# A two-layer S5 and convolution decoder on one core: the mixer's products in another order, weight units queued one unit later

## The chip, the core and the metric

The kernel runs on one core of one Trainium2 chip. The metric is the device time of one execution in microseconds, as the median of three runs; smaller is better.

## The reference

Two layers are computed for 288 tokens (256 of a prompt, 8 x 4 of a decode batch), with D_MODEL 2048, all in float32. The part that the change touches is the mixer of each layer:

```python
z = x @ w_in                                   # 2048 -> 1024 (u) + 1024 (cv) + 1024 (cg)
u, cv, cg = z[..., :1024], z[..., 1024:2048], z[..., 2048:]
y5, h_re, h_im = _s5(u, ...)                   # 64 groups x 16 channels, complex state of 64
g5 = gelu(y5)
s5_out = g5 * sigmoid(g5 @ s5_w_glu)
c = cv * sigmoid(cg)
c, new_conv = _causal_dwconv(c, conv_buf, conv_w, conv_b)     # width 31, per channel
c = silu(_ln(c, conv_ln_g, conv_ln_b))
mix = concatenate([s5_out, c]) @ w_out
x = _ln(ALPHA * x + mix, ln1_g, ln1_b)
```

A convolutional feed-forward net (2048 to 11264 and back) and an embedding product with layer norms follow. They are not changed.

## The kernel before

**Products.** Channels lie on the partitions, tokens on the free axis: x is 16 tiles of 128 x 288. Every weight matrix is cut into blocks of 128 x 128, stored in the order of use, and a block is used by three matmuls of 288 columns, since float32 is made of two halves: weight-high by x-high (L369), weight-high by x-low (L374), weight-low by x-high (L375). The first blocks of a group go in an order that uses the low halves last (L371, L351). `_order(matrix, ms, ks, g)` lists the blocks of a product for output chunks ms over input chunks ks, with g output chunks side by side for the first group; `run` (L343) walks such a list, and evicts an accumulator EV_GAP blocks after it is complete.

**Weights.** Eight blocks are a unit of 512 KB. `stream_dma` (L174) loads a unit into one of RAW_BUFS = 4 buffers `wraw`, on SP's queue (L179); `stream_hi` (L183) copies the high half to `whi` on ACT (L195); `stream_lo` (L199) makes `wlo` = wraw - whi on DVE and then queues the load of unit s + RAW_BUFS. This load can start when its buffer is free, that is after the `wlo` of the unit four before it. All operations of DVE are recorded in one line, L140, so the text goes by their tiles.

**The mixer** (L1051) computes first four chunks of u (phase u0), then for j = 0 to 7: the pair of cv and cg chunk j (phase p{j}, 32 blocks), the convolution of chunk j - 1 (`conv`, L1096), the DMAs for the convolution of chunk j (`stack`, L1070), and, where U_AT names one, one further chunk of u (phase v{j}, 16 blocks). A conv chunk goes through memory: DVE writes the gated product to `cbuf` (one buffer), POOL's queue writes cbuf to `cb_d` (L1136) and, after it, reads it back shifted in four DMAs into `stack` (L1078; the last chunk's on SP's queue), writes cbuf to the output (`out_dram`, L1080), and then loads the cached columns of the next chunk into cbuf (L1115). The convolution is 64 small matmuls on `stack` and `cw` (L1105, L1108).

**The scan** of the S5 runs beside this, chunk by chunk, as generators that `tick` steps between blocks. A chunk of u goes to memory (`u_d`) and comes back as `ust` (L799); `make_e` builds `em` from `sqb`, `sbt` and others (DVE, ACT); `bu` = ust by em and `project` = ust by tm and hin by om are small matmuls (both L389); between them kp goes to `k_d` and comes back as `tm` (L876); the result y goes to `y_d` and comes back in another order (L968), for the gelu. Loads are on SP's queue, which also carries the weights. When the generators step is decided when the program is built, by a model of TensorE's time: `pe_t` grows by 369 ns for each block and by 640 ns for each of a convolution's eight steps.

**The end of the mixer** is the glu product g (64 blocks; cut by G_CUT so that 32 blocks run ahead of the last convolution, 8 and 24 more beside its layer norm), then conv(7) and its layer norm (`ln_finish`, whose last matmul is L510, on the tile `ln_dg`), then the out product o: 256 blocks with 16 input chunks, k 0 to 7 from the scan and k 8 to 15 from the convolution, five output chunks side by side first.

Of the kernel before, what the change touches and what calls it, by code (L numbers as in the profile page):

```python
# [7 lines left out]
F32 = mybir.dt.float32  # L8
# [5 lines left out]
P = 128  # L14
# [12 lines left out]
CVC = 8  # L27
# [38 lines left out]
LOOK = 1  # L66
EV_GAP = 10
NATIVE = 10
G_CUT = (32, 40, 64, 64)
U_AT = {1: [4], 2: [5], 3: [6], 4: [7]}  # L70

# [22 lines left out]
def layer_phases():  # L94
    ph = [("u0", _order("w_in", range(4), range(KD), 4))]
    for j in range(CVC):
        ph.append((f"p{j}", _order("w_in", [8 + j, 16 + j], range(KD), 0)))
        if j in U_AT:
            ph.append((f"v{j}", _order("w_in", U_AT[j], range(KD), 0)))
    ph.append(("g", _order("s5_w_glu", range(8), range(8), 4)))  # L100
    ph.append(("o", _order("w_out", range(KD), range(KD), 5)))
    for z, ms in enumerate(EPARTS[:3]):
        ph.append((f"e{z}", _order("pe_w", ms, range(PEK), 0)))
    j0 = 0
    for h, n in enumerate(FH):
# [48 lines left out]
class Core:  # L154
# [44 lines left out]
    def stream_lo(self, upto):  # L199
        upto = min(upto, self.nblk // SB - 1)  # L200
        while self.next_lo <= upto:
# [8 lines left out]
            self.next_lo += 1  # L210
            self.stream_dma(s + RAW_BUFS)

# [129 lines left out]

    def run(self, blocks, xs, evac, sums=None, wide=False):  # L343

# [3 lines left out]
        for _, k, m in blocks:  # L348
# [17 lines left out]
            else:  # L366
                xh, xl = xs(k)
                self.pe_t += 369.0
                nc.tensor.matmul(out, w[0], xh, start=first, stop=False)  # L369
# [7 lines left out]
            if last:  # L377
                a, t = accs.pop(m)
                self.evq.append((a, lambda m=m, t=t: evac(m, t[:, :TOK])))
            if self.evq and self.pos - self.ev_pos >= EV_GAP:  # L380
                self.evict()
# [669 lines left out]
    def mixer(self, l, ph):  # L1051
        nc, a = self.nc, self.a
        V = self.V
        with self.tc.tile_pool(name="mx", bufs=1) as mp:
# [34 lines left out]
            def split_g(force=False, n=S5C):  # L1089
                while n and self.gdone and (force or self.gdone[0][1] <= self.pe_t):  # L1090
                    c = self.gdone.pop(0)[0]
                    self.split_x(8 + c, self.u32[c])
                    gsplit.add(c)
                    n -= 1

            def conv(j):  # L1096
                st, cw = stacks.pop(j)
                o = self.acc_tile()
                for k in range(8):
                    self.tick()  # L1100
                    self.pe_t += 640.0
                    if j == CVC - 2 and k >= 4:
                        split_g(n=1)
                    for b in range(4):
# [42 lines left out]

            def xs_g(k):
                split_g()
                while k not in gsplit:  # L1150
                    self.step(scan)
                    self.run_timed(True)
                    split_g(True)
                return self.xh[8 + k], self.xl[8 + k]
            def ev_g(m, acc):
                t = mp.tile([P, TOK], F32, tag="cvt", name="gt", bufs=3)
                nc.scalar.activation(t, acc, AF.Tanh, scale=0.25)
                w = mp.tile([P, TOK], F32, tag="cvt", name="gt", bufs=3)
                V.scalar_tensor_tensor(w.rearrange("p (n s) -> p s n", s=STEP),
                                       t.rearrange("p (s n) -> p s n", s=STEP), 1.0,  # L1160
                                       self.u32[m].rearrange("p (s n) -> p s n", s=STEP), op0=OP.add, op1=OP.mult)
                self.split_x(m, w, 0.25)
            sums = self.sums(ph["g"])
            self.run(ph["g"][:G_CUT[0]], xs_g, ev_g, sums)
            self.finish(scan)
            conv(CVC - 1)

            def fill(z):
                self.run(ph["g"][G_CUT[z]:G_CUT[z + 1]], xs_g, ev_g, sums)
            fill(0)  # L1170
            self.flush()
            self.ln_finish(cst, lambda z: z and fill(z), keep=True)
            th = {}

# [7 lines left out]
            def c_silu(j):  # L1182
# [4 lines left out]
                                          (3, lambda j: self.split_lo(8 + j, cvo[j], 0.5)))))  # L1187
            if G_CUT[2] < G_CUT[3]:
                fill(2)
            self.load_p(l, mp)  # L1190
            st = self.ln_begin(DM)

            def xs_o(k):
                self.need(min(k - 3, 7) - LOOK)
                return self.xh[k], self.xl[k]

            def ev_o(m, acc):
                V.scalar_tensor_tensor(self.x32[m], self.x32[m], 1.0 if m == KD - 1 else ALPHA, acc,
                                       op0=OP.mult, op1=OP.add)
                self.ln_acc(st, self.x32[m], m == KD - 1)  # L1200
                if m == 6:
                    self.ln_pre(st, self.x32[KD - 1], ALPHA)
            self.run(ph["o"], xs_o, ev_o, wide=True)
        return st

# [308 lines left out]
```

## Time and profile before

| | us |
|---|---|
| median of 3 runs | 2790.59 (2786.01 to 2801.34) |
| the profiled execution, its own time | 2793.7 |
| its span | 2791.9 |
| busy in the span: PE | 2684.0 (96%) |
| DVE | 1815.6 (65%) |
| ACT | 1353.2 (48%) |
| POOL | 304.3 (11%) |

The profiled execution has 1.8 us outside its span and is 3.1 us above the median. The profile is a page (busy time, 40 slices of the span, the chain that ended last, the costliest groups) and a trace that answers queries by window, engine and tile. Matmuls are pipelined, so the recorded duration of one (0.29 us) is longer than the distance between two. A wait is put down to whatever released it last.

### The profile page before, as it was taken

To read this page: it belongs to the slowest core of one execution; us is meant where nothing else is said; L and a number is where in the kernel's file an instruction comes from. 1 tells how busy PE (TensorE), PEld (TensorE's weight loads), DVE (VectorE), ACT (ScalarE), POOL (GpSimd) and SP (SyncE) were. 2 spreads that over 40 slices of the span, in tenths; PEclk is the share of its full clock that TensorE was granted. 3 is DMA by queue.
4 is the path that set the end of the run, shared out by engine and by line. 5 is a ranking of instruction groups with operands and counts; after the bars stand their busy time and mean duration, and the time that the engine had idled before them with its cause. 6 is when DMAs were issued, how large, how long until landed. Compare 5 with 4: busy or idle time off the path is not lost. (4 is left out here: it accounts for less than half of the span.)

```text
span 2791.9 us, 57891 instructions
## 1 busy us (share of the span) xinstructions
PE 2684.0 (96%) x23696; PEld 2623.0 (94%) x23696; DVE 1815.6 (65%) x3017; ACT 1353.2 (48%) x2224; POOL 304.3 (11%) x923
## 2 busy tenths in 40 slices
PE   8889999999999999999889879999999999999997
PEld 7778999999999999999888769999999999999997
DVE  6875768664566456667778747676645664566686
ACT  3444547553455345536454435475534553455363
POOL 3442001000000000000115410010000000000000
PEclk9999999999999999999999999999999999999998
DMA  7887544554455544544468874445555455455543
GB/s 238 240 237 224 171 152 164 162 181 163 158 168 164 180 159 157 181 162 151 145 197 242 225 206 156 150 161 165 180 166 162 159 179 171 150 173 171 166 152 102
DMA packets 175609, 487.72 MB, mean 175 GB/s; under 512 B 37616, under 2 KB 61696, under 8 KB 175344
## 3 DMA queue, kind: packets, MB, share of 16 engines
q1 hardware_dynamic: 160832, 434.56, 48.6%
q0 software_dynamic: 14512, 49.47, 6.4%
q8 instruction: 186, 3.05, 0.4%
q14 instruction: 79, 0.65, 0.1%
HBM read 463.27 MB, written 20.68 MB: 173 GB/s over the span
## 5 line engine op out<-in xcount | busy, mean ns | idle before, releaser
L369 PE MATMUL acc<-xh,whi 128*128 128x288 f32 x4656 | 1389.3, 299 | 13.0 <-ACT xh L528 5.1
L374 PE MATMUL acc<-xl,whi 128*128 128x288 f32 x4357 | 1289.7, 296 | 0.6 <-DVE xl L140 0.2
L375 PE MATMUL acc<-xh,wlo 128*128 128x288 f32 x4357 | 1284.3, 295 | 0.5 <-issue 0.5
L195 ACT ACTIVATE whi<-wraw 128x1024 fp32r<-128x1024 f32 x766 | 791.4, 1050 | 350.5 <-PE acc L374 220.4
L140 DVE TENSOR_TENSOR wlo<-wraw,whi 128x1024 fp32r<-128x1024 f32 x766 | 918.6, 1223 | 28.6 <-issue 12.5
L369 PEld LDWEIGHTS acc<-xh,whi 128*128 128x128 f32 x4656 | 876.5, 188 | 20.5 <-ACT xh L528 5.4
L374 PEld LDWEIGHTS acc<-xl,whi 128*128 128x128 f32 x4357 | 821.4, 189 | 3.7 <-DVE xl L140 2.1
L375 PEld LDWEIGHTS acc<-xh,wlo 128*128 128x128 f32 x4357 | 823.8, 189 | 0.7 <-issue 0.7
L140 DVE SCALAR_TENSOR_TENSOR fo<-fe,parf,fo 128x304 f32<-128x304 f32 x352 | 188.2, 535 | 354.2 <-ACT fo L1250 347.9
L369 PE MATMUL acc<-hh,whi 128*128 128x288 f32 x1408 | 416.4, 296 | 0.0
L374 PE MATMUL acc<-hl,whi 128*128 128x288 f32 x1312 | 387.7, 296 | 0.0
L375 PE MATMUL acc<-hh,wlo 128*128 128x288 f32 x1312 | 387.4, 295 | 0.0
L369 PEld LDWEIGHTS acc<-hh,whi 128*128 128x128 f32 x1408 | 264.9, 188 | 0.1
L375 PEld LDWEIGHTS acc<-hh,wlo 128*128 128x128 f32 x1312 | 247.2, 188 | 0.0
L374 PEld LDWEIGHTS acc<-hl,whi 128*128 128x128 f32 x1312 | 247.0, 188 | 0.0
L1246 ACT ACTIVATE fe<-acc 128x256 f32<-128x256 f32 x176 | 67.6, 384 | 301.1 <-PE acc L375 301.1
L1256 POOL COPY fstage<-fe 128x9 f32<-128x9 f32 x176 | 42.2, 240 | 1035.3 <-ACT fe L1247 1024.5
L428 ACT ACTIVATE ln_q<-x 128x288 f32<-128x288 f32 x90 | 40.2, 446 | 221.0 <-DVE x L140 221.0
L140 DVE TENSOR_TENSOR x<-x,acc 128x288 f32<-128x288 f32 x64 | 29.1, 454 | 144.7 <-PE acc L375 144.7
L1250 ACT ACTIVATE fo<-fe,parf 128x304 f32<-128x304 f32 x176 | 113.0, 642 | 16.5
L1270 ACT ACTIVATE hh<-fth 128x288 fp32r<-128x288 f32 x88 | 39.2, 445 | 162.9 <-DVE fth L140 162.9
L140 DVE SCALAR_TENSOR_TENSOR x<-x,acc 128x288 f32<-128x288 f32 x64 | 29.0, 453 | 132.9 <-PE acc L375 132.9
(237 smaller groups left out, 2366.9 us busy)
## 6 DMA issues: line engine op xcount, KB each, us to landing
wraw<-in_wts_dram SPq DMA_DIRECT2D x776, 512.0 KB
stack<-cb_d POOLq DMA_DIRECT2D x56, 282.0 KB, 8.8
cw<-in_convw_dram POOLq DMA_DIRECT2D x16, 512.0 KB, 5.7
cbuf<-in_convi_dram POOLq DMA_DIRECT2D x16, 283.5 KB, 4.5
cb_d<-cbuf POOLq DMA_DIRECT2D x16, 283.5 KB, 4.0
out_dram<-cbuf POOLq DMA_DIRECT2D x16, 283.5 KB, 10.4
tm<-k_d SPq DMA_DIRECT2D x64, 64.0 KB
sbt<-in_s5b_dram SPq DMA_DIRECT2D x14, 256.0 KB
```

The lines of the kernel that those rows point to most:

```text
L140: return f(out, *args, **kw)
L195: self.nc.scalar.activation(hi, self.raw[s], AF.Copy)
L369: nc.tensor.matmul(out, w[0], xh, start=first, stop=False)
L374: nc.tensor.matmul(out, w[0], xl, start=False, stop=False)
L375: nc.tensor.matmul(out, w[1], xh, start=False, stop=last)
L428: nc.scalar.activation(st["q"], v, AF.Square)
L1246: nc.scalar.activation(e[:, 2:2 + SEQ], acc[:, :SEQ], AF.Copy)
L1250: nc.scalar.activation(o[:, :w], e[:, 2:EW], AF.Identity, bias=self.prm("ffn_conv_b", m), scale=self.prm("ffn_conv_w2", m))
L1256: nc.gpsimd.tensor_copy(stage[:, z, :, 0], e[:, SEQ:EW:6])
L1270: nc.scalar.activation(hh[i], h, AF.Copy, scale=0.5)
```

## The change

The numbers of U_AT move two of the four u chunks that are computed between conv chunks one place forward (chunk 4 to j = 0, chunk 5 to j = 2) and the other two back (chunk 6 to j = 7, chunk 7 behind the last convolution, its first four blocks ahead of the layer norm's matmuls and twelve beside them). The out product is split: `oc` (input chunks 8 to 15, from the convolution, all output chunks, into ALPHA * x + result) runs right behind the convolution's layer norm, then g whole, then `os` (input chunks 0 to 7, added to x). The halves swap their tiles: the scan's chunks are split into tiles 0 to 7 for g, the glu's results into 8 to 15. HALF_GAP = 6 sets the evictions of oc and os. A weight unit is queued behind the `wlo` of the unit three before it, one unit later than before; its buffer comes free with the `wlo` of the unit four before it, as before. The model's `pe_t` grows by 400 ns for a block and 500 ns for a step of a convolution.

```diff
-G_CUT = (32, 40, 64, 64)
-U_AT = {1: [4], 2: [5], 3: [6], 4: [7]}
+HALF_GAP = 6
+U_AT = {0: [4], 2: [5], 7: [6]}
+U_END = 7
+V_CUT = (0, 4)
...
+    ph.append(("vz", _order("w_in", [U_END], range(KD), 0)))
+    ph.append(("oc", _order("w_out", range(KD), range(8, KD), 4)))
     ph.append(("g", _order("s5_w_glu", range(8), range(8), 4)))
-    ph.append(("o", _order("w_out", range(KD), range(KD), 5)))
+    ph.append(("os", _order("w_out", range(KD), range(8), 5)))
...
-            self.stream_dma(s + RAW_BUFS)
+            self.stream_dma(s + RAW_BUFS - 1)
...
-                self.pe_t += 369.0
+                self.pe_t += 400.0
...
-                    self.split_x(8 + c, self.u32[c])
+                    self.split_x(c, self.u32[c])
...
-                    self.pe_t += 640.0
-                    if j == CVC - 2 and k >= 4:
-                        split_g(n=1)
+                    self.pe_t += 500.0
...
+            conv(CVC - 1)
+            self.run(vz[V_CUT[0]:V_CUT[1]], self.xs, ev_u, vsum)
+            self.flush()
+            self.ln_finish(cst, lambda z: z and self.run(vz[V_CUT[1]:], self.xs, ev_u, vsum), keep=True)
...
+            def xs_c(k):
+                self.need(k - 8)
+                return self.xh[k], self.xl[k]
+
+            def ev_c(m, acc):
+                V.scalar_tensor_tensor(self.x32[m], self.x32[m], ALPHA, acc, op0=OP.mult, op1=OP.add)
+            self.run(ph["oc"], xs_c, ev_c, gap=HALF_GAP)
...
-            sums = self.sums(ph["g"])
-            self.run(ph["g"][:G_CUT[0]], xs_g, ev_g, sums)
+                self.split_x(8 + m, w, 0.25)
+            self.run(ph["g"], xs_g, ev_g)
             self.finish(scan)
-            conv(CVC - 1)
...
-            self.run(ph["o"], xs_o, ev_o, wide=True)
+            self.run(ph["os"], lambda k: (self.xh[8 + k], self.xl[8 + k]), ev_s, wide=True, gap=HALF_GAP)
```

SP's queue in layer 0, around the loads for the third chunk's scan (`wraw` a weight unit, `tm`, `sbt`, `sqb` the scan's tables, `u` the way back of y), before:

```order
L179 DMA wraw<-in_wts_dram 128x1024 x3
L876 DMA tm<-k_d 32x4x128 x4
L776 DMA sbt<-in_s5b_dram 128x512
L785 DMA sqb<-q_d 128x1x128 x4
L968 DMA u_2_182<-y_d 32x4x72 x4
```

and now:

```order
L183 DMA wraw<-in_wts_dram 128x1024 x2
L880 DMA tm<-k_d 32x4x128 x4
L183 DMA wraw<-in_wts_dram 128x1024
L780 DMA sbt<-in_s5b_dram 128x512
L789 DMA sqb<-q_d 128x1x128 x4
L972 DMA u_2_182<-y_d 32x4x72 x4
```

One of the three weight units that stood ahead of `tm` stands behind it.

SP's queue at the end of the same mixer, from the scan's sixth chunk on (`stack` is the last convolution's input), before:

```order
L968 DMA u_5_185<-y_d 32x4x72 x4
L179 DMA wraw<-in_wts_dram 128x1024 x3
L876 DMA tm<-k_d 32x4x128 x4
L179 DMA wraw<-in_wts_dram 128x1024
L968 DMA u_6_186<-y_d 32x4x72 x4
L179 DMA wraw<-in_wts_dram 128x1024 x4
L968 DMA u_7_187<-y_d 32x4x72 x4
L1078 DMA stack<-cb_d 32x4x564 x4
L179 DMA wraw<-in_wts_dram 128x1024 x8
```

and now:

```order
L972 DMA u_5_185<-y_d 32x4x72 x4
L183 DMA wraw<-in_wts_dram 128x1024 x5
L1082 DMA stack<-cb_d 32x4x564 x4
L183 DMA wraw<-in_wts_dram 128x1024 x4
L803 DMA ust<-u_d_3378 32x4x72 x4
L183 DMA wraw<-in_wts_dram 128x1024 x3
L803 DMA ust<-u_d_3552 32x4x72 x4
L183 DMA wraw<-in_wts_dram 128x1024 x6
L880 DMA tm<-k_d 32x4x128 x4
L183 DMA wraw<-in_wts_dram 128x1024 x2
L972 DMA u_6_186<-y_d 32x4x72 x4
```

The scan's last two chunks moved from ahead of the last `stack` to behind it.

DVE in layer 0, the last rows up to `xl_118`, the low half of the last conv chunk, which is the last input of its kind that the out product waits for (`cvo` a conv chunk, `ln_d` its normalised form, `xl` low halves; `sw`, `pw`, `bsm` tables of the scan), before:

```order
L140 TENSOR_TENSOR ln_d<-cvo_195,ln_s_4152 128x288
L140 SCALAR_TENSOR_TENSOR cvo_194<-ln_d,cvo_194 128x288
L140 SCALAR_TENSOR_TENSOR xl_116<-cvo_193,xh_100 128x288
L140 SCALAR_TENSOR_TENSOR cvo_195<-ln_d,cvo_195 128x288
L140 SCALAR_TENSOR_TENSOR xl_117<-cvo_194,xh_101 128x288
L140 TENSOR_TENSOR wlo<-wraw,whi 128x1024
L140 SCALAR_TENSOR_TENSOR xl_118<-cvo_195,xh_102 128x288
```

and now:

```order
L144 SCALAR_TENSOR_TENSOR cvo_194<-ln_d,cvo_194 128x288
L144 SCALAR_TENSOR_TENSOR xl_116<-cvo_193,xh_100 128x288
L144 TENSOR_TENSOR sw<-scc,aP 128x512 x2
L144 SCALAR_TENSOR_TENSOR cvo_195<-ln_d,cvo_195 128x288
L144 SCALAR_TENSOR_TENSOR xl_117<-cvo_194,xh_101 128x288
L144 TENSOR_TENSOR pw<-sw 128x4x64
L144 SCALAR_TENSOR_TENSOR pw<-sw 128x4x64
L144 TENSOR_TENSOR sw<-sbc,q 128x128 x2
L144 TENSOR_TENSOR bsm<-sw 64x4x16 x4
L144 TENSOR_TENSOR wlo<-wraw,whi 128x1024
L144 TENSOR_TENSOR sw<-bu,stb 128x576 x2
L144 SCALAR_TENSOR_TENSOR xl_118<-cvo_195,xh_102 128x288
```

Operations of the scan's last two chunks stand between the conv chunks now (four more, on `sqb` and `sw`, a little ahead of these rows); before, the scan was over here.

## Rows read from the trace of the kernel before

**Rows 1.** The page, busy time: engine, us, share of the span, instructions.

```profile
PE 2684.0 (96%) x23696; PEld 2623.0 (94%) x23696; DVE 1815.6 (65%) x3017; ACT 1353.2 (48%) x2224; POOL 304.3 (11%) x923
```

**Rows 2.** Windows: length, busy PE, PEld, DVE, ACT, POOL, clock, DMA share, GB/s.

```profile
61.00:306.00 245.00, 217.24 (x3511) 197.27 (x3512) 172.37 (x308) 104.52 (x199) 83.73 (x154) 0.97 0.80 230
600.00:1100.00 500.00, 500.00 (x3754) 500.00 (x3753) 277.94 (x383) 229.64 (x348) 23.92 (x146) 1.00 0.52 167
1392.00:1700.00 308.00, 268.80 (x3847) 245.34 (x3846) 214.44 (x383) 141.58 (x260) 90.19 (x165) 0.93 0.73 206
```

**Rows 3.** PE's waits from 1390 to 1700: us in total, times, the longest.

```profile
PE y L389 <- DMA wraw<-in_wts_dram: 7.6, 1, 7.6
PE acc L1105 <- DMA stack<-cb_d: 7.4, 1, 7.4
...
PE bu L389 <- DMA ust<-u_d: 5.2, 1, 5.2
PE acc L369 <- ACT xh L528: 5.1, 1, 5.1
PE y L389 <- DMA tm<-k_d: 3.1, 1, 3.1
PE bu L389 <- ACT em L815: 3.0, 3, 2.5
```

**Rows 4.** PE's waits from 55 to 306 (columns as in rows 3).

```profile
PE bu L389 <- ACT em L815: 8.4, 7, 3.6
PE bu L389 <- DMA ust<-u_d: 6.0, 2, 3.4
...
PE acc L1105 <- DMA stack<-cb_d: 2.1, 2, 1.3
```

**Rows 5.** Windows behind stalls (columns as in rows 2).

```profile
144.50:148.90 4.40, 4.09 (x72) 3.72 (x73) 4.32 (x13) 1.82 (x4) 0.58 (x1) 0.61 0.59 181
205.80:210.30 4.50, 4.50 (x102) 4.30 (x103) 1.60 (x3) 1.32 (x3) 1.57 (x3) 0.50 1.03 283
1455.60:1459.60 4.00, 4.00 (x66) 2.31 (x68) 2.75 (x5) 0.85 (x2) 1.09 (x2) 0.50 0.72 239
1640.30:1643.90 3.60, 3.60 (x98) 3.40 (x99) 0.00 (x0) 0.49 (x2) 0.47 (x1) 0.50 0.70 221
1668.40:1674.60 6.20, 6.19 (x52) 4.36 (x56) 3.29 (x7) 2.41 (x7) 0.00 (x0) 0.50 0.04 15
```

**Rows 6.** Timeline of SP's queue: start, us, instruction.

```profile
192.94 0.33 SPq L179 DMA_DIRECT2D wraw<-in_wts_dram  x1
193.37 2.06 SPq L876 DMA_DIRECT2D tm<-k_d  x4
```

**Rows 7.** Timeline of PE: start, us, instruction, idle time before and its end.

```profile
205.78 0.47 PE L389 MATMUL y<-ust,tm 128*32 128x72 f32 x8 [5.71 <-DMA sqb<-q_d]
...
281.26 0.64 PE L1105 MATMUL acc<-stack,cw 128*32 128x256 f32 x8 [1.29 <-DMA stack<-cb_d]
```

**Rows 8.** One convolution alone, by the tile stack (columns as in rows 2).

```profile
262.00:266.30 4.30, 4.17 (x128) 2.68 (x128) 0.00 (x0) 0.00 (x0) 0.00 (x0) 1.00 0.60 188
```

**Rows 9.** Timeline of POOL's queue, layer 0 (columns as in rows 7).

```profile
247.19 0.56 POOL L1136 DMA_DIRECT2D cb_d<-cbuf  x1 [4.78 <-DVE cbuf L140]
...
263.60 0.56 POOL L1115 DMA_DIRECT2D cbuf<-in_convi_dram  x1 [9.60 <-DMA out_dram<-cbuf]
...
267.94 0.54 POOL L1136 DMA_DIRECT2D cb_d<-cbuf  x1 [2.72 <-DVE cbuf L140]
```

**Rows 10.** Timeline of DVE behind the conv's layer norm (as in rows 7).

```profile
308.34 2.35 DVE L140 TENSOR_TENSOR wlo<-wraw,whi 128x1024 fp32r<-128x1024 f32 x2
310.61 0.82 DVE L140 TENSOR_TENSOR cvo<-cvo,ln_s 128x288 f32<-128x288 f32 x2
...
328.80 0.45 DVE L140 SCALAR_TENSOR_TENSOR xl<-cvo,xh 128x288 fp32r<-128x288 f32 x1
```

**Rows 11.** A group of DVE by shape, 61 to 306: busy us, mean ns.

```profile
L140 DVE TENSOR_TENSOR sw<-scc,aP 128x512 f32<-128x512 f32 x14 | 9.3, 692 | 14.6 <-DMA scc<-in_s5c_dram 13.3 <-ACT em L815 1.1
```

More of the change, by code (lines that the diff above doesn't have):

```diff
@@ L341, in sums, with run @@
         return tot, {m: 0 for m in tot}, {}
-    def run(self, blocks, xs, evac, sums=None, wide=False):
+    def run(self, blocks, xs, evac, sums=None, wide=False, gap=EV_GAP):
         nc = self.nc
@@ L379, in run @@
                 self.evq.append((a, lambda m=m, t=t: evac(m, t[:, :TOK])))
-            if self.evq and self.pos - self.ev_pos >= EV_GAP:
+            if self.evq and self.pos - self.ev_pos >= gap:
                 self.evict()
@@ L1146, in mixer @@
                     self.run(ph[f"v{j}"], self.xs, ev_u)
[L1148 to L1162, printed above, removed]
-            sums = self.sums(ph["g"])
-            self.run(ph["g"][:G_CUT[0]], xs_g, ev_g, sums)
-            self.finish(scan)
+            vz = ph["vz"]
+            vsum = self.sums(vz)
             conv(CVC - 1)
-            def fill(z):
-                self.run(ph["g"][G_CUT[z]:G_CUT[z + 1]], xs_g, ev_g, sums)
-            fill(0)
+            self.run(vz[V_CUT[0]:V_CUT[1]], self.xs, ev_u, vsum)
             self.flush()
-            self.ln_finish(cst, lambda z: z and fill(z), keep=True)
+            self.ln_finish(cst, lambda z: z and self.run(vz[V_CUT[1]:], self.xs, ev_u, vsum), keep=True)
             th = {}
@@ L1187, in mixer, with xs_g, ev_g, ev_s @@
                                           (3, lambda j: self.split_lo(8 + j, cvo[j], 0.5)))))
-            if G_CUT[2] < G_CUT[3]:
-                fill(2)
+            def xs_c(k):
[4 more added lines that the diff above has]
+            self.run(ph["oc"], xs_c, ev_c, gap=HALF_GAP)
+            def xs_g(k):
+                split_g()
+                while k not in gsplit:
+                    self.step(scan)
+                    self.run_timed(True)
+                    split_g(True)
+                return self.xh[k], self.xl[k]
+            def ev_g(m, acc):
+                t = mp.tile([P, TOK], F32, tag="cvt", name="gt", bufs=3)
+                nc.scalar.activation(t, acc, AF.Tanh, scale=0.25)
+                w = mp.tile([P, TOK], F32, tag="cvt", name="gt", bufs=3)
+                V.scalar_tensor_tensor(w.rearrange("p (n s) -> p s n", s=STEP),
+                                       t.rearrange("p (s n) -> p s n", s=STEP), 1.0,
+                                       self.u32[m].rearrange("p (s n) -> p s n", s=STEP), op0=OP.add, op1=OP.mult)
+                self.split_x(8 + m, w, 0.25)
+            self.run(ph["g"], xs_g, ev_g)
+            self.finish(scan)
             self.load_p(l, mp)
             st = self.ln_begin(DM)
[L1193 to L1199, printed above, removed]
+            def ev_s(m, acc):
+                V.tensor_tensor(self.x32[m], self.x32[m], acc, OP.add)
                 self.ln_acc(st, self.x32[m], m == KD - 1)
                 if m == 6:
-                    self.ln_pre(st, self.x32[KD - 1], ALPHA)
-            self.run(ph["o"], xs_o, ev_o, wide=True)
+                    self.ln_pre(st, self.x32[KD - 1])
+            self.run(ph["os"], lambda k: (self.xh[8 + k], self.xl[8 + k]), ev_s, wide=True, gap=HALF_GAP)
         return st
```

## The prediction

> **What bounds the kernel now.** I read the busy times first. PE is busy for 2684.0 of the 2791.9 us of the span [rows 1], so all waits of TensorE together are 108 us, and no reordering can bring more than these and what the clock loses behind them. Next the windows: from 600 to 1100, in the feed-forward net, PE is busy throughout, 3754 matmuls in 500 us, 0.133 us each, so a block of three takes 0.40 us and a weight unit 3.2 us [rows 2]. The two mixers are different: 27.8 us idle of 245 in layer 0 and 39.2 of 308 in layer 1, with a DMA share of 0.80 and 0.73 against 0.52, and DVE busy for 70% of both [rows 2]. 67 of the 108 us lie there, and that is where the change works. Third, what the waits are for: loads and tables of the scan (ust, tm, em), the conv stack, and in layer 1 the scan's last chunk [rows 3, 4]. Fourth, the clock: behind a stall of some 3 us or more, PE runs for a few us at its lower level, a granted clock of 0.50 (1.2 of 2.4 GHz), in layer 1 from 1455.6, 1640.3 and 1668.4, in layer 0 from 205.8, and in part (0.61) from 144.5 [rows 5]. A stretch of 4.0 us at 0.50 costs 2.0 us more.
>
> **What it takes away.** Same matmuls, in another order; the terms are waits.
>
> *The first convolution of layer 1* waits 7.4 us for its stack [rows 3]. Chunk 4 of u now stands ahead of it, 16 blocks of 0.40, 6.4 us of cover; with the clock behind the stall, 2.0, that is 8.4.
>
> *The scan's last two chunks in layer 1* wait 3.1 (tm), 7.6 (put down to a weight load, at the project of the last chunk) and 5.1 (g for the last xh) [rows 3]. They now run beside oc, where 128 blocks, 51 us, stand between the last u and g, and no conv traffic runs. I take all of it, 15.8, with the clock behind two of them, 1.8 and 3.1 [rows 5]: 20.7.
>
> *Weight units one place later.* On SP's queue in layer 0 a weight load went out at 192.94 and tm right behind it, at 193.37 [rows 6]; the project that needed the loads began at 205.78, after 5.71 us of idle time [rows 7]. With one unit fewer ahead of it a load goes out up to 3.2 us earlier. I take 3.2 of that stall, 2.8 of the em waits of layer 0 (a third of 8.4: the tables' loads are behind weights too) [rows 4], 2.5 of em in layer 1 and 1.8 of its ust wait of 5.2 [rows 3], with the clock of two windows, 2.2 and 1.7 [rows 5]: 14.2. Lower end: nothing, if the transfers and not the queue are late. Upper end: all these waits. That weights then run dry I cost at nothing: three units still wait ahead of PE's, 9.6 us, and a load's buffer comes free at the same moment as before.
>
> The SP queue is one reading; the other is the DMA engines themselves. They were 0.80 busy on average [rows 2] and 1.03 in the window in which PE resumed [rows 5], and the load issued at 193.37 was needed at 205.78, 12 us later. The Trainium skill, "Trainium Kernel Development and Optimization", Key Constraints, says that DMAs of all queues run on the same 16 engines and interleave, so that issuing them otherwise saves only issue time; by that rule the 14.2 would be near nothing and the sum 14 us higher.
>
> *The last two convolutions of layer 0* waited 2.1 [rows 4]: gone as such, replaced below. Taken away in all: 8.4 + 20.7 + 14.2 + 2.1 = 45.4.
>
> **What it adds.**
>
> *The conv chunks' round through memory.* cbuf is one buffer. Its round is 20.75 us, from cb_d at 247.19 to the next at 267.94, of which 9.60 are a wait for the write to the output [rows 9]. A convolution starts 14.8 us behind its cb_d (262.0, [rows 8, 9]); the last, whose stack is on SP, 13.3 behind it (281.26, [rows 7, 9]). PE has 32 blocks and a convolution between two, 12.8 + 4.2 [rows 8], 17.0 us. Before, u chunks and the scan's products lay between; now nothing is left from conv(4) on but v7. With cb_d of chunk 5 at 0, about 1.4 behind the end of p5 (an estimate: two evictions and the gating), the next two go out at 20.75 and 41.5. PE ends conv(4), p6, conv(5) and p7 at 32.6 and waits until 35.6 for conv(6): 3.0. Then conv(6) and v7 end at 46.2, and conv(7) can start at 54.8: 8.6. In layer 1 I count the last alone, 8.4, since conv(4) and conv(5) lie some 4 us further apart there by the scan's products. With half speed for 4 us behind each long stall: 20.0 + 4.0 = 24.0. Lower end, from the same rows, if the output write lands in 6 us instead of 9.6: 14. Upper end: 30, if layer 1 has all that layer 0 has.
>
> *The head of oc.* Before, the out product began with eight input chunks of the scan, long ready; now its first 32 blocks need all eight conv chunks, each after four DVE operations. In the trace DVE took from 310.61 to 329.25 for them, 18.6 us with five `wlo` between [rows 10]. Now three `wlo` stand there (1.18 each, half of 2.35 [rows 10]): 16.3. But 16 operations of the scan stand there too in layer 0, six of 512 columns or more at 0.69 [rows 11], ten of half that or less at about 0.35: 7.6. Two `wlo` stand ahead, so DVE begins 1.8 us behind the layer norm's last matmul, and the last low half is there 25.7 us after it. PE has 0.5, 28 blocks (11.2) and 32 small matmuls (0.06 each, as eight took 0.47 [rows 7]), 13.6. So it waits 12.1 in layer 0, and 10.7 in layer 1, where the two reads of bu stand later: 22.8. The stall comes in pieces of one or two us per chunk, so I add no clock. Lower end: the first chunk's latency alone, 5.5 a layer, 11. Upper end: 27, with half speed for 4 us in each layer on top.
>
> *At nothing:* the layer norm's small operations (12 blocks of vz, 4.8 us, hide a chain of less than that); the changed evictions (HALF_GAP), one DVE operation each as before; the start of g, whose last input is due 204 matmuls, 27 us, behind the last project by the order; os, which has all its inputs when g is evicted, in the order of its use. Without their cover each would cost 1 to 5 us a layer.
>
> **The sum.** +24.0 + 22.8 - 45.4 = +1.4 us. The profiled execution took 2793.7, so 2795.1; that execution is 3.1 above the median, which gives **2792**. No change, since 0.5% (14 us) is about what a measurement can tell.
>
> **The rivals.**
>
> A, *the scan's queue was the whole matter*: with the weights out of the way the rest of its waits goes too: 2.5 of the tm wait, 6.0 ust, 5.6 em, 3.4 ust in layer 1 and some 4 of clock, 21.5. Then 2770. For it: SP is held by weight loads that wait for `wlo` just ahead of late loads [rows 6]. Against: DVE, 70% busy, makes em itself.
>
> B, *the transfers, not the queue* (slower): the scan's loads land as late as before because the DMA engines are full, so the 14.2 doesn't come, while the new waits do, and a unit fewer ahead gives nothing back: 2806. It decides where the time from a load's issue to the scan's matmul stays at 12 us or grows. For it: 1.03 in [rows 5]. Against: a mean of 0.80 leaves a fifth.
>
> C, *the new waits are half as long*: oc starts each chunk as it comes (11 instead of 22.8), and the output write lands sooner in a quiet stretch (14 instead of 24): 22 less, 2770. For it: no scan runs beside p5 to p7. Against: weights at 167 GB/s [rows 2] and the stack's reads share the engines there too.
>
> That the change doesn't do what it says: the order shows that it does.
>
> **How the numbers follow.** Forecast 0.42, A 0.18, B 0.26, C 0.14. The forecast and its terms' errors spread by some 12 us either way. Faster by over 0.5%: most of A and C and a little of the forecast, 0.32. Slower: most of B and a little of the forecast, 0.24. Within: 0.44. Range: down to A's and C's time less a few us, 2763, up to B and half a term, 2813.
>
> **What would show it.** Right: PE's waits for the stack of 8 us at the last convolution in each layer, and 10 us or more on xl in the first 32 blocks of oc, with DVE without a gap there; no wait of g for xh; conv(0) of layer 1 without a stall; bu and project waits smaller by a unit's time. Wrong: the sum fails if waits on ust, tm and em stay as they are, if oc's head waits under 6 us, or if weights (`whi`, `wlo`) show as PE's releasers in the mixers.

## The result and the profile after

The changed kernel takes 2836.28 us (median of 4 runs, 2835.36 to 2840.51); the kernel before, run beside it, 2794.14 (4 runs). The ratio is 1.0155, 95% interval [1.0122, 1.0187]: 42 us slower, where no change was forecast and 2813 was the upper end.

The page of the changed kernel, busy time (for [rows 1]); its span is 2833.5 us:

```profile
PE 2697.6 (95%) x23696; PEld 2634.5 (93%) x23696; DVE 1820.6 (64%) x3049; ACT 1353.0 (48%) x2224; POOL 303.7 (11%) x923
```

Idle time of PE grew from 107.9 to 135.9 us, and its busy time by 13.6, for the same matmuls: that part is clock. What PE waits for, over the whole span (us in total, times, the longest; for [rows 3, 4]):

```profile
PE acc L1107 <- DMA stack<-cb_d: 35.9, 8, 8.6
PE bu L393 <- ACT em L819: 12.8, 10, 5.5
...
PE y L393 <- DMA tm<-k_d: 9.5, 3, 4.6
PE acc L373 <- ACT xh L532: 8.1, 2, 4.0
PE bu L393 <- DMA tm<-k_d: 6.2, 1, 6.2
...
PE acc L378 <- DVE xl L144: 5.3, 3, 2.9
PE acc L1107 <- issue: 4.9, 2, 3.5
PE lnp L463 <- DVE ln_s L144: 4.7, 2, 2.4
```

The waits for the stack are now 35.9, with 4.9 more put down to "issue" at the same line; before they were 7.4 and 2.1. The scan's waits in layer 1 that the change aimed at, 7.6, 3.1 and 5.1, and the first convolution's 7.4 are gone as forecast. New are the waits for `xh` (twice 4.0, the first conv chunk of oc), for `xl` (in the head of oc) and for `ln_s`. The scan's waits on tm are 15.7 now (9.5 and 6.2), where the kernel before has 4.0, and those on em 12.8 against 11.4; only those on ust fell, from 11.1 to 1.7. The prediction had named unchanged waits on ust, tm and em as a sign that its sum fails: for tm and em it came.

A window of the changed kernel (columns as in rows 2): three rounds of the run of conv chunks at the end of layer 0's mixer, without u chunks between them ("bare run" below):

```profile
183.00:256.00 73.00, 58.28 (x775) 51.94 (x771) 28.58 (x47) 23.15 (x39) 20.65 (x38) 0.88 0.81 222
```

Where the conv chunks follow each other, PE is busy 58.3 of 73 us at a clock of 0.88, though DVE is busy for only 28.6 and the DMA share is 0.81. So no compute engine bounds it, and on average the DMA engines are not full either.

The stages can be cut at the last matmul of a layer norm, which all versions have. The tile `ln_dg`, before (acc is the conv layer norm, lnp the others; first and last start at the end of each line):

```profile
L510 PE MATMUL lnp<-ln_dg,ones x12: 406/510/847, 415.3 to 2775.5; 96*128 96x288 f32 x12
L510 PE MATMUL acc<-ln_dg,ones x4: 403/404/406, 302.8 to 1693.5; 96*128 96x288 f32 x4
```

and after:

```profile
L514 PE MATMUL lnp<-ln_dg,ones x12: 406/510/850, 444.2 to 2817.5; 96*128 96x288 f32 x12
L514 PE MATMUL acc<-ln_dg,ones x4: 403/405/407, 284.5 to 1689.5; 96*128 96x288 f32 x4
```

In layer 0 the conv layer norm comes at 302.8 before and 284.5 after, the one behind the out product at 415.3 and 444.2. Between the two cuts 31.5 us of work moved: g, 64 blocks of 0.40, 25.6, and 336 small matmuls of two scan chunks. These pass PE much faster than the 0.06 that eight took in [rows 7]:

```profile
296.46 1.21 PE L393 MATMUL bu<-ust,em 128*32 128x72 f32 x64
297.60 0.40 PE L373 MATMUL acc<-xh,whi 128*128 128x288 f32 x1
```

64 of them hold back the next block by 1.1 us, the 96 of a project by 1.6; all 336 take 5.9. With the same cuts in layer 1 (1388.6, 1693.3, 1805.8 before; 1417.5, 1689.3, 1847.8 after), the account is:

| stretch | before | after | due after, from before and the work that moved | lost |
|---|---|---|---|---|
| layer 0, 55 to the conv layer norm | 247.8 | 229.5 | 216.3 | 13.2 |
| layer 0, conv layer norm to the next | 112.5 | 159.7 | 144.0 | 15.7 |
| layer 1, its start to the conv layer norm | 304.7 | 271.8 | 273.2 | -1.4 |
| layer 1, conv layer norm to the next | 112.5 | 158.5 | 144.0 | 14.5 |

The sum, 42.0, is the whole difference of the spans (41.6). 30.2 of it lie behind the conv layer norm, in the stretch of oc, g and os ("the out product" below), and 11.8 ahead of it; in layer 1 the waits that went, 23.2 us (15.8 of the scan and 7.4 of the first convolution), are in the -1.4, so nearly as much was lost there to other waits.

**The conv round.** POOL's queue in layer 0 (start, us, instruction, idle before and its end; for [rows 9]):

```profile
207.74 0.54 POOL L1138 DMA_DIRECT2D cb_d<-cbuf  x1 [3.13 <-DVE cbuf L144]
...
231.30 0.54 POOL L1138 DMA_DIRECT2D cb_d<-cbuf  x1 [3.97 <-DVE cbuf L144]
...
235.18 2.20 POOL L1082 DMA_DIRECT2D stack<-cb_d  x4 [2.80 <-DMA cb_d<-cbuf]
...
251.78 0.56 POOL L1117 DMA_DIRECT2D cbuf<-in_convi_dram  x1 [13.85 <-DMA out_dram<-cbuf]
255.91 0.54 POOL L1138 DMA_DIRECT2D cb_d<-cbuf  x1 [3.57 <-DVE cbuf L144]
```

A round of cbuf takes 23.6 and 24.6 us (207.74 to 231.30 to 255.91), not 20.75, since the output write lands only 11.9 and 13.9 us after POOL begins to wait for it. What else goes out at that time shows on SP's queue:

```profile
230.73 1.73 SPq L972 DMA_DIRECT2D u<-y_d  x4
232.56 9.47 SPq L183 DMA_DIRECT2D wraw<-in_wts_dram  x5
```

SP had been held by the load of y until 230.73; then weight units go out one behind the other from 232.56 on, just ahead of the stack's reads at 235.18. The windows around (columns as in rows 2):

```profile
218.00:225.00 7.00, 5.61 (x46) 5.40 (x48) 0.04 (x1) 1.06 (x1) 0.00 (x0) 1.00 1.03 277
243.00:250.00 7.00, 0.00 (x0) 0.00 (x0) 1.23 (x1) 2.23 (x3) 0.00 (x0) 0.64 0.98 255
250.20:256.00 5.80, 5.80 (x104) 3.49 (x108) 0.92 (x3) 0.00 (x0) 0.66 (x2) 0.57 0.24 78
```

Ahead of PE's wait for the stack and in it the DMA engines are at 1.03 and 0.98; behind it they are at 0.24, and PE's clock is 0.57 (about its lower level, 1.2 of 2.4 GHz). The engines are full in bursts. What they move while full depends on the transfers; two more windows of this trace:

```profile
1618.00:1622.00 4.00, 4.00 (x31) 4.00 (x31) 0.00 (x0) 0.42 (x2) 0.13 (x1) 1.00 1.09 230
1673.00:1677.00 4.00, 4.00 (x68) 2.26 (x68) 0.00 (x0) 0.00 (x0) 0.00 (x0) 0.50 1.02 416
```

**The end of os.** One output chunk on DVE (start, us, instruction):

```profile
428.75 1.22 DVE L144 TENSOR_TENSOR wlo<-wraw,whi 128x1024 fp32r<-128x1024 f32 x1
...
431.77 0.45 DVE L144 TENSOR_TENSOR x<-x,acc 128x288 f32<-128x288 f32 x1
432.14 1.22 DVE L144 TENSOR_TENSOR wlo<-wraw,whi 128x1024 fp32r<-128x1024 f32 x1
```

From one `wlo` to the next 3.4 us pass, full of five operations of 288 columns (four are cut out here); PE delivers an output chunk of os every 3.2 (8 blocks). Before, an output chunk of o was 16 blocks, 6.4 us. So DVE falls behind over 16 chunks, and PE waits for the last sums:

```profile
434.27 1.21 PE L463 MATMUL lnp<-ones_d,ln_s 128*96 128x1 f32 x12 [2.32 <-DVE ln_s L144]
```

**The head of oc**, PE's timeline in layer 0:

```profile
289.17 0.48 PE L373 MATMUL acc<-xh,whi 128*128 128x288 f32 x1 [4.03 <-ACT xh L532]
...
307.94 0.40 PE L378 MATMUL acc<-xl,whi 128*128 128x288 f32 x1 [2.92 <-DVE xl L144]
```

4.03 for the first chunk, then 0.82 and 2.92 for low halves, 7.8 in all; in layer 1 4.0 and 1.6. From 289.2 to 293.0 the clock is 0.55.

### The profile page after: what moved, and what is told of

Its sections match the earlier page's. It is cut to its first block, busy times and chain, and to the rows that moved or that the text cites. A ratio compares the mean times of both kernels' runs of the same rounds, so it can differ in the third digit from the quotient of the medians.

```text
span 2833.5 us, 57988 instructions
## 1 busy us (share of the span) xinstructions
PE 2697.6 (95%) x23696; PEld 2634.5 (93%) x23696; DVE 1820.6 (64%) x3049; ACT 1353.0 (48%) x2224; POOL 303.7 (11%) x923
## 5 line engine op out<-in xcount | busy, mean ns | idle before, releaser
L373 PE MATMUL acc<-xh,whi 128*128 128x288 f32 x4656 | 1390.1, 299 | 14.5 <-ACT xh L532 8.1
L378 PEld LDWEIGHTS acc<-xl,whi 128*128 128x128 f32 x4325 | 814.8, 188 | 10.7 <-DVE xl L144 7.9
L144 DVE TENSOR_TENSOR x<-x,acc 128x288 f32<-128x288 f32 x96 | 43.3, 451 | 151.3 <-PE acc L379 151.3
L1107 PE MATMUL acc<-stack,cw 128*32 128x256 f32 x1024 | 79.9, 432 | 40.8 <-DMA stack<-cb_d 35.9
## 6 DMA issues: line engine op xcount, KB each, us to landing
out_dram<-cbuf POOLq DMA_DIRECT2D x16, 283.5 KB, 11.7
```

The lines of the kernel that those rows point to most:

```text
L144: return f(out, *args, **kw)
L378: nc.tensor.matmul(out, w[0], xl, start=False, stop=False)
L1107: nc.tensor.matmul(o[32 * b:32 * b + 32, :SEQ], cw[:, b, k], st[:, b, 4 * k:4 * k + SEQ], start=(k == 0), stop=False, tile_position=(0, 32 ...
```

## Experiments

Five theories were told apart. *Late weights*: with a unit fewer ahead weights run dry. *Ring*: cbuf's single buffer holds POOL's queue, with it y_d, with it SP. *Chain*: the latency of cb_d, stack and output write by itself. *Bandwidth*: the DMA engines are full, and each byte costs time. *Head*: the split of the out product costs by itself. The experiments ran in four groups (1 to 4; 5 to 8; 9 to 11; 12 to 14), and the kernel before took 2794.0 to 2797.4 beside them, so a difference between two groups is uncertain by about 3 us.

### 1 and 2. The weights' place in the queue, undone and alone

```diff
-            self.stream_dma(s + RAW_BUFS - 1)
+            self.stream_dma(s + RAW_BUFS)
```

in the changed kernel; and the reverse in the kernel before.

> The change with weight units queued as before (one unit earlier); all else of the change stays. Theory Late weights: the unit fewer ahead is what makes the convolutions wait, so the stack waits of conv 6 and 7 (8.1 and 6.1 in layer 0, 8.6 and 5.7 in layer 1) fall by half and the time to about 2815. Theory Ring (cbuf is one buffer, so POOL's queue waits some 12 us for the output write, behind it the scan's y_d, behind that SP's load of y and the weights, which then go out in a bunch with the next stack): the queueing of one unit hardly matters, 2836 within 7. Theory of the prediction (SP's queue order gives the scan 14): 2850.

Measured: 2842.5 (2837.8 to 2849.1), 1.0173 [1.0154, 1.0191] of before; 6 slower than the change, with intervals that overlap. The waits of conv 6 and 7 fall from 28.5 to 23.1 (7.0, 5.1, 4.7 and 6.3), not by half, and the time does not fall at all. Of the three forecasts Ring's, 2836 within 7, just holds; the prediction's term, inside the change, does not.

> The kernel before with weight units queued one unit later, nothing else. The prediction's term: 14 us faster than before, 2780, with tm and em waits shorter by 3 each. Theory Late weights: slower, 2805 or more, with waits for the stack or for wlo and whi. Theory Ring: neither, 2794 within 7, since the waits come from what blocks the queue (y_d, wlo), not from the place of one unit.

Measured: 2781.63 (2776.42 to 2788.28), 0.9954 [0.9937, 0.9971], 13 faster than before. Late weights falls; the prediction's term, 14, holds as a number when it stands alone. SP's queue in this kernel at the place of [rows 6]:

```profile
186.41 1.80 SPq L876 DMA_DIRECT2D tm<-k_d  x4
```

tm goes out at 186.41, 7 us earlier than before, and the project's wait of 5.71 [rows 7] is gone. But layer 0's mixer as a whole did not get faster. By the cuts at `ln_dg` (this kernel's lines stand in experiment 5) its stretch ahead of the conv layer norm takes 252.0 us, before 247.8: waits on em there are 10.5 instead of 8.4, on the stack 5.4 instead of 2.1. In layer 1 the same stretch takes 288.8 instead of 304.7. Two profiles of one kernel (experiments 7 and 10) differ by 0.9 and 3.6 us in these stretches. So the gain lies in layer 1, and over the whole kernel the waits on tm and em did not get shorter by 3 each, as expected, but longer (5.5 and 14.0 instead of 4.0 and 11.4). The new order costs the loss of 42 and this gain too: 2781.6 to 2836.3, 55 us.

### 3 and 4. Two buffers for cbuf

```diff
-                cb = mp.tile([P, CBW], F32, tag="cbuf", name="cbuf", bufs=1)
+                cb = mp.tile([P, CBW], F32, tag="cbuf", name="cbuf", bufs=2)
```

> The change with two buffers for cbuf, so the next chunk's gating waits for no output write. Theory Ring: POOL's waits for out_dram go, the stack waits of conv 6 and 7 fall from 28.5 in both layers to under 10, and with the clock behind them the time to 2805 to 2815. Theory Bandwidth (weights and conv traffic, 4.5 MB per 17 us of products, fill the DMA engines): the waits stay over 20, time above 2828.

Measured: 2811.52 (2808.07 to 2816.31), 1.0063 [1.0045, 1.008]; 25 faster than the change. PE's waits in it:

```profile
PE acc L1107 <- DMA stack<-cb_d: 22.2, 7, 4.8
...
PE acc L1107 <- issue: 8.3, 3, 6.2
```

30.5 instead of 40.8 (32.3 with 1.8 at the convolution's other line): the second buffer takes away a part of these waits, the rest stays, as Bandwidth said; the time, 2811.5, is Ring's and not Bandwidth's. The step by which Ring explained it fails: SP's wait for y_d, from 55 to 290, in the change and here:

```profile
SPq L972 <- DMA y_d<-yw: 28.7, 4, 10.8
```

```profile
SPq L972 <- DMA y_d<-yw: 27.3, 4, 12.9
```

28.7 and 27.3. The second buffer lets cb_d go out earlier; it doesn't free y_d. But with it the DMA engines stand idle less: in the same three rounds of the bare run they are now at 0.87 and 241 GB/s, and the rounds take 68 us; the change with one buffer has 0.81, 222 and 73.

```profile
176.00:244.00 68.00, 57.36 (x776) 51.05 (x779) 27.89 (x47) 24.08 (x42) 21.01 (x37) 0.93 0.87 241
```

> The kernel before with two buffers for cbuf. Theory Ring: the scan's waits that stand behind y_d in the queues shrink, 5 to 15 faster than before (2780 to 2789). Theory Bandwidth: no difference, 2794 within 5.

Measured: 2793.36 (10 runs, 2788.72 to 2801.03), 0.9998 [0.9985, 1.0011]. No difference: in the old order, with the weights early, the round did not bind.

### 5. The split of the out product alone

```diff
-            self.run(ph["o"], xs_o, ev_o, wide=True)
+            self.run(ph["oc"], xs_c, ev_c, gap=HALF_GAP)
...
+            self.run(ph["os"], lambda k: (self.xh[k], self.xl[k]), ev_s, wide=True, gap=HALF_GAP)
```

on the kernel of experiment 2, with the changed kernel's phases and evictions for oc and os; g, scan and u stay where they were.

> The kernel before with weights one unit later (2782 measured) and, of the mixer's new order, only the split of the out product: oc right behind the conv layer norm, then os; the scan, g and the u chunks stay where they were. Theory Head: DVE's 18 us for eight conv chunks against 13 of PE, and its 3.3 us per output chunk in os against PE's 3.2, cost by themselves: some 6 at the head and 2.4 at the layer norm behind os, each with the clock, in both layers, 17 together: 2799. Theory Scan beside it: the waits at oc's head come from the scan's operations that run there in the change; alone, the split costs 5 or less: 2787.

Measured: 2812.27 (6 runs, 2807.09 to 2815.82), 1.0053 [1.0036, 1.0069]; 30.6 slower than without the split. The cuts at `ln_dg`, without the split and with it:

```profile
L510 PE MATMUL lnp<-ln_dg,ones x12: 406/510/847, 419.5 to 2763.9; 96*128 96x288 f32 x12
L510 PE MATMUL acc<-ln_dg,ones x4: 403/404/406, 307.0 to 1681.8; 96*128 96x288 f32 x4
```

```profile
L512 PE MATMUL lnp<-ln_dg,ones x12: 404/511/849, 431.7 to 2795.2; 96*128 96x288 f32 x12
L512 PE MATMUL acc<-ln_dg,ones x4: 403/404/406, 302.4 to 1699.9; 96*128 96x288 f32 x4
```

From the conv layer norm to the next, layer 0 takes 129.3 instead of 112.5; layer 1 125.9 instead of 112.5. The two, 30.2, are nearly all of the difference, and the same 30.2 as in the changed kernel. PE's timeline in layer 0 shows two waits (start, us, idle before):

```profile
309.54 0.61 PE L371 MATMUL acc<-xh,whi 128*128 128x288 f32 x1 [6.45 <-ACT xh L530]
```

```profile
417.50 1.85 PE L461 MATMUL lnp<-ones_d,ln_s 128*96 128x1 f32 x12 [2.34 <-DVE ln_s L142]
```

and the window behind the second (columns as in rows 2):

```profile
418.00:432.00 14.00, 14.00 (x63) 13.32 (x63) 5.70 (x19) 4.46 (x9) 0.20 (x1) 0.52 0.25 90
```

A wait of 6.45 for the first conv chunk (4.03 in the changed kernel; here DVE and ACT still evict the last glu chunk, until 304.8, before they turn to the conv chunks), and one of 2.34 for the layer norm's sums. Layer 1 has the same two waits. Behind the second PE ran at 0.52 for 14 us, through the layer norm's products and the blocks between them: from the first of its sums to `ln_dg` the same matmuls take 14.2 us here and 8.3 in the kernel without the split, 6.0 more, over twice the wait itself (3.1 more in layer 1). Head is right in kind; the size, 17, was underestimated through the clock. Scan beside it falls: no scan runs there, and the split alone costs as much as in the change.

### 6 and 9. Fewer bytes

cw, the convolution's weights as blocks of 32 x 32 for TensorE, is 0.5 MB per conv chunk.

```diff
-                cw = mp.tile([P, 4, 8, 32], F32, tag="cw", name="cw", bufs=1)
-                nc.gpsimd.dma_start(cw, a["convw"][l, j])
+                if j == 0:
+                    cw = mp.tile([P, 4, 8, 32], F32, tag="cw", name="cw", bufs=1)
+                    nc.gpsimd.dma_start(cw, a["convw"][l, j])
+                    cws.append(cw)
+                cw = cws[0]
```

> The change with two cbuf (2811 measured), and cw, 0.5 MB of weights per conv chunk, loaded for the first chunk of a layer only; the other convolutions use the first chunk's weights, so that part is left out. Theory Bandwidth: a conv chunk's share of the engines' time falls by 0.5 of 4.5 MB, some 2 us per chunk; the stack waits fall from 33 in both layers to under 20 and the time to 2798 or less. Theory Chain: the wait is the latency of cb_d, stack and queue, which cw does not lengthen: waits over 27, 2808 or more.

Measured: 2783.07 (2781.26 to 2784.63), 0.9948 [0.9931, 0.9966]: 28.4 faster than experiment 3. The stack waits:

```profile
PE acc L1110 <- DMA stack<-cb_d: 14.5, 7, 4.7
```

14.5 and 0.9 at this line, where 30.5 stood. The bare run shows why: three rounds take 60 us instead of 68, at the same rate as in experiment 3.

```profile
172.00:232.00 60.00, 54.27 (x775) 49.72 (x779) 28.14 (x47) 23.92 (x41) 19.28 (x34) 0.99 0.86 246
```

14.8 MB instead of 16.4, at 246 and 241 GB/s: with two buffers the bytes set the pace of the bare run. Bandwidth, not Chain.

> The change itself (one cbuf) with cw loaded for the first chunk of a layer only; the other convolutions use its weights, so that part is left out. With two cbuf the same edit gave 28. Theory Bandwidth alone: 28 here too, 2808. Theory Both (a round of one cbuf is a chain of transfers, each as long as the engines are full): the round of cbuf shortens by some 2 us but still holds the last two convolutions, 10 to 20 faster, 2816 to 2826. Theory Chain alone: 2831 or more.

Measured: 2807.58 (2805.71 to 2808.25), 1.005 [1.0033, 1.0066]: 28.7 faster than the change with the same single buffer. In total that is Bandwidth again. But in the bare run of layer 0 the round of cbuf did not shorten: 24.3 and 23.4 us, where the change has 23.6 and 24.6.

```profile
197.97 0.54 POOL L1141 DMA_DIRECT2D cb_d<-cbuf  x1 [3.94 <-DVE cbuf L144]
...
222.31 0.54 POOL L1141 DMA_DIRECT2D cb_d<-cbuf  x1 [3.31 <-DVE cbuf L144]
...
245.72 0.54 POOL L1141 DMA_DIRECT2D cb_d<-cbuf  x1 [3.28 <-DVE cbuf L144]
```

The first of these three goes out 9.8 us earlier than in the change: in layer 0 most of the gain came ahead of the bare run, beside the scan. The round itself still takes what it took, which theory Both expected in part; its time, 2816 at the least, did not come. The bytes, in the change and here:

```profile
DMA packets 175609, 487.72 MB, mean 172 GB/s; under 512 B 37616, under 2 KB 61696, under 8 KB 175344
```

```profile
DMA packets 173593, 480.38 MB, mean 171 GB/s; under 512 B 37392, under 2 KB 61472, under 8 KB 173328
```

7.34 MB fewer, 28.7 us: 256 GB/s. The other transfers got shorter (issue to landing, median, in the change and here):

```profile
stack<-cb_d POOLq DMA_DIRECT2D x56, 282.0 KB, 9.6
```

```profile
stack<-cb_d POOLq DMA_DIRECT2D x56, 282.0 KB, 8.0
```

The output writes fell from 11.7 to 9.0. A rival is the place of cw's load: it stands ahead of the stack's reads on POOL's queue and waits for the convolution before it. But from cb_d to these reads 5.0 us pass on average in the change and 4.8 here, so that place isn't what was saved. Whether the same bytes would cost as much on another queue was not tried.

### 7 and 10. Later weights and two buffers in the old order

> The kernel before with weights one unit later and two cbuf. If what holds the scan's loads is the ring through cbuf's output write, then with the weights out of the way it gains 5 more: 2776. If two cbuf only helped the change's bare run of conv chunks: 2782 within 5.

Measured: 2776.82 (5 runs, 2770.94 to 2784.84), 0.9932 [0.9909, 0.9955].

> The kernel before with weights one unit later and two cbuf, again, in more rounds: 2777 within 4 if the 17 to 20 that it gained are real, ratio 0.993 within 0.002; 2782 if the second buffer adds nothing to the later weights.

Measured: 2777.03 (6 runs, 2773.22 to 2779.15), 0.9939 [0.9923, 0.9954]. 17 faster than before, 5 better than the weights alone; that the second buffer gives these 5 is likely, with intervals that still touch.

### 8. One u chunk at its new place

```diff
-U_AT = {1: [4], 2: [5], 3: [6], 4: [7]}
+U_AT = {0: [4], 2: [5], 3: [6], 4: [7]}
```

on the kernel of experiment 2. (Chunk 5 stands at j = 2 in both kernels, so of the places that the change gives to u only chunks 4, 6 and 7 are new.)

> The kernel before with weights one unit later, and of the change's new places for u only the first: chunk 4 at j = 0 instead of 1. The first convolution of layer 1 waits 4.2 in the run without it. Prediction's term: that wait and the clock behind it go, 6 faster: 2776. Rival: the scan of the next chunks meets the convolutions elsewhere, and the same waits appear one place on: 2782 within 5.

Measured: 2799.42 (10 runs, 2790.11 to 2803.52), 0.9995 [0.998, 1.0011]: 18 slower than without it (11 by the two ratios to the kernel before). The first convolution of layer 1 no longer waits, but PE's waits from 1390 to 1720 read

```profile
PE y L389 <- DMA tm<-k_d: 12.5, 3, 9.1
PE bu L389 <- ACT em L815: 11.3, 5, 8.9
```

where experiment 2 had 5.3 and 3.5. The rival holds, and more than it said: with cover added in front of one transfer, the scan's waits came back one place on. That these met a busier moment is likely and not shown.

### 11. What the bytes cost in the old order

> The same with cw loaded once per layer (the other convolutions use the first chunk's weights: left out). If full DMA engines hold back the scan's loads too: 10 or more faster, 2767. If the engines bind only where conv chunks follow each other without u or scan between: 2774 within 3.

Measured: 2750.16 (2747.86 to 2753.07), 0.9846 [0.9828, 0.9863]: 26.9 faster than experiment 10. The bytes count in the old order just as much, so it is not the bare run of conv chunks alone, and cw's bytes are not what makes the new order slower than the old. PE's waits for ust, a load on SP's queue, fall from 11.6 to 2.5.

### 12 to 14. The same bytes saved without leaving work out

The blocks of cw are zero but for their diagonals. Here 16 KB per chunk are loaded, and the blocks made on the chip:

```diff
-                nc.gpsimd.dma_start(cw, a["convw"][l, j])
...
+                w0, e0 = cwps[j // 4][:, 32 * (j % 4):32 * (j % 4) + 32], self.eye[:, :]
+                nc.gpsimd.tensor_tensor(cw.rearrange("p b k c -> p (b k) c"),
+                                 bass.AP(tensor=w0.tensor, offset=w0.offset, ap=[list(w0.ap[0]), [1, 32], [0, 32]]),
+                                 bass.AP(tensor=e0.tensor, offset=e0.offset, ap=[list(e0.ap[0]), [0, 32], [1, 32]]),
+                                 OP.mult)
```

> The kernel before with weights one unit later and two cbuf (2777 measured), and cw built on the chip: 16 KB per chunk are loaded instead of 0.5 MB, and POOL multiplies them by an identity of 32 columns, 128x1024. All is computed. Theory Bandwidth: the 27 of the run that left cw out come here too, less what POOL's product delays on its queue: 2750 to 2758. Rival: POOL's product takes several us, holds the scan's DMAs behind it, and the gain is under 10: 2768 or more.

Measured: 2760.29 (2754.23 to 2761.13), 0.9875 [0.9857, 0.9893]: 17 faster than experiment 10, just past the forecast's end: 10 of the 27 are lost again with the product on POOL. The product, of this kernel (durations, shortest, median, longest):

```profile
L1088 POOL TENSOR_TENSOR cw<-cwp,eye x16: 1917/1932/2194, 67.1 to 1621.6; 128x1024 f32<-128x1024 f32 x16
```

> The same with the product on DVE (some 1.2 us each like wlo, 16 of them, 20 in both layers, on an engine 70% busy in the mixers). Bandwidth: 2750 to 2762, DVE's share costing a few. Rival: DVE's backlog delays em, kp and wlo as much as the loads gain: 2770 or more.

Measured: 2747.81 (2745.7 to 2751.73), 0.9837 [0.982, 0.9853]: 46 faster than before, and the fastest of all that compute everything. The diff is the same but for `V.tensor_tensor`. DVE's product:

```profile
L140 DVE TENSOR_TENSOR cw<-cwp,eye x16: 1211/1224/1683, 57.0 to 1610.3; 128x1024 f32<-128x1024 f32 x16
```

So the 27 of experiment 11 come from the bytes: a version that computes all gains 29. DVE's 16 operations of 1.22, 20 us on an engine that is 70% busy in the mixers, cost nothing that shows.

> The change with two cbuf (2811) and cw built on POOL. Bandwidth: 2783 to 2790, like the run that left cw out, so the change's order stays some 30 slower than the old order with the same DMA traffic, of which the split of the out product is 20 or more.

Measured: 2790.94 (10 runs, 2781.19 to 2798.87), 0.9987 [0.9972, 1.0002], just past the forecast's end. At the same traffic the new order is 31 slower than the old one (2760.29).

**The two orders side by side.** The cuts at `ln_dg` in four pairs of kernels that differ in the order alone, the weights one unit late in all. In us, for both layers together, "ahead" from 55 in layer 0 and from layer 1's start to the conv layer norm; the 63.0 of work that moved (31.5 a layer) are put back:

| pair (old order, new order) | ahead, old | ahead, new, +63.0 | out product, old | out product, new, -63.0 |
|---|---|---|---|---|
| one buffer (experiment 2, the change) | 540.8 | 564.3 | 225.1 | 255.2 |
| two buffers (10, 3) | 537.5 | 536.6 | 225.1 | 258.1 |
| two buffers, cw once (11, 6) | 511.6 | 509.0 | 225.1 | 258.0 |
| two buffers, cw built on POOL (12, 14) | 518.7 | 518.2 | 225.0 | 258.0 |

The out product costs 30 to 33 more in the new order in every pair. Ahead of it the new order costs 23.5 more with one buffer and nothing with two. So the 55 us are the split of the out product, some 30, and the ring of cbuf's one buffer, some 25; in the old order a second buffer gave nothing (experiment 4) or 5 (7 and 10). The bytes of cw are worth 28 in either order and are no part of the difference. The changed constants of the model (`pe_t`) were not tried by themselves; what they do is in these sums.

## Why the prediction was wrong

In the prediction's terms, what stands ahead of the out product was to gain 21.4 (24.0 - 45.4) and lost 11.8; the out product was to lose 22.8 and lost 30.2.

*The conv chunks' round*, 24.0, upper end 30: this step failed. The mechanism was right (conv 6 and conv 7 wait in both layers, and a second buffer, which takes the round away, gives 25), the size was not. Conv 6 and conv 7 wait 28.5 instead of 20.0, and all convolutions together 40.8 where the kernel before has 10.4, with the clock behind them. That eats what the new order takes away: with two buffers the new order gains nothing ahead of the out product against the old, and with one it loses 23.5 (the pairs above). I took the round, 20.75, and the 14.8 from cb_d to the convolution from the one round of the trace that ran beside other work, and carried them into a stretch where nothing but conv chunks and products was to run. There the rounds were 23.6 and 24.6, with 11.9 and 13.9 of wait for the output write instead of 9.6, and even with two buffers three rounds take 68 us, 22.7 each, not PE's 17.0. The sum needed a second line beside the chain of latencies, bytes over rate. Counted by hand a round is 2 MB of weights and 2.5 MB of the conv chunk; in the trace it is 5.5 MB, since the scan's loads go on (16.4 MB in the three rounds), at 241 GB/s. That the bytes count is shown (6, 9, 11, 13), and that the one buffer costs 25 in this order (3, and the pairs); that the weights held behind y_d and then sent in a bunch make conv 6's wait longer is read from the queues and was not tried.

*The head of oc*, 22.8: too large, and in part for the wrong reason. The waits at the head are 7.8 in layer 0 and 5.6 in layer 1 (4.0 and 1.6), not 12.1 and 10.7: in layer 0 the last low half was there 23.2 us behind the layer norm's last matmul (284.7 to 307.94), not 25.7, and PE itself needed 15.5 up to there (23.2 less the waits of 7.8), not 13.6, since behind the first wait it ran at 0.55. I added no clock because the stall would come in pieces; the first piece was 4.0. The "stall of some 3 us" that I set for the clock is no border: the 2.3 us at the end of os were followed by 0.69.

*At nothing: os.* This step failed too. I named the evictions as one DVE operation each as before, and looked at inputs; but an output chunk now comes every 3.2 us, not 6.4, and DVE needs 3.4 for its sums and one `wlo`. It makes 2.3 us of wait in each layer, and 1.7 more with the clock behind it (6.0 in layer 0 of experiment 5). The start of g, at nothing too, waits 1.0 in each layer. With the head these waits are 20 of the 30.2 that the out product lost; most of the rest is PE at a lower clock behind them.

*The weights' place in the queue*, 14.2: the number was right for the kernel before, 13, and that was partly luck. The stall that I named first went (tm 7 us earlier), but 9.9 of my 14.2 lay in layer 0, whose mixer got 4.2 slower; the gain, 15.9, came in layer 1, where I had counted 4.3. Inside the change the term is worth 6 at most, with intervals that overlap. Rival B, that the engines and not the queue hold these loads, falls for the kernel before, where the place of one unit alone gave 13. The Trainium skill says in "Trainium Kernel Development and Optimization", Key Constraints, that DMAs from the queues of SP, ACT and POOL all run on the same 16 DMA engines. Experiment 11 agrees: bytes taken off POOL's queue shortened PE's waits for ust, on SP's queue, from 11.6 to 2.5. What the Trainium skill says there of issue time is about issuing from several engines at once; the prediction applied it to a place within one queue, and there experiment 2 decides.

*Taken away.* The waits of layer 1 that were to go, 15.8 and the 7.4 of the first convolution, went. But others came back at the stack and at em. Experiment 8 shows the same in small: 6 forecast for moving one u chunk, 11 to 18 lost.

So the result lies on rival B's side, and beyond its 2806, but not by B's mechanism: the loss is the split and the ring.

## What to carry to other kernels

When work is moved out of a stretch, redo both lines for what remains: the chain of transfers through the fewest buffers, and the bytes over the rate of a loaded stretch of the same mix (here 241 to 246 GB/s; single full windows gave 230 to 416). A latency taken from a trace holds at that trace's load. A product that is cut in two along its inputs delivers outputs twice as often in its second half: set the eviction's work against the new interval. To find where a reordering lost its time, cut both kernels at marks that both have, count the work that moved in the trace, and compare pairs that differ in the order alone. And look for bytes that can be made on the chip: here 8 MB of mostly zero blocks, made on DVE, were worth 29 us, more than any reordering gave.

## What the hardware showed that was not expected

A mean DMA share of 0.80 and 0.73 in the two mixers [rows 2] did not mean free room: 7.34 MB fewer gave 26.9 us in the old order and 28.7 and 28.4 in the new one, with one buffer and with two, 256 to 273 GB/s. A wait of 2.34 us ahead of a layer norm was followed by 14 us at a clock of 0.52 in layer 0 of experiment 5; in the changed kernel nearly the same wait (2.32) was followed by 5.5 us at 0.69. The same matmuls took 14.2 and 9.9 us there, and 8.3 without the wait. The same product of 128x1024 took 1.93 us on POOL and 1.22 on DVE, and although DVE is the busier engine, the kernel with it on DVE is 12 us faster.
